# Every fourth expert weight tile split on GpSimd instead of VectorE

## The chip, the cores and the metric

The kernel runs on one core of one Trainium2 chip. The metric is the device time of one execution in microseconds (us); lower is better. A difference of 0.2% (about 4 us) is about what a measurement of this kernel can tell from no change.

Engines, as the profile names them: PE is TensorE (PEld its weight load), DVE is VectorE, ACT is ScalarE, POOL is GpSimd, SP is SyncE, whose queue issues the loads.

## The reference

A decoder trunk of two layers on 256 tokens of width 1024. Each layer has a mixer (a convolution with attention in layer 0, a sparse attention in layer 1) and then a mixer of experts. The experts are where the change lies:

```python
def peer_ffn(h, w_q, sub_keys, u, v):
    ...
        q = (xc @ w_q).reshape(-1, PEER_HEADS, 2, half)
        s = jnp.einsum('thpd,pkd->thpk', q, sub_keys).astype(jnp.float32)
        sv, si = lax.top_k(s, PEER_TOPK)
        ...
        cv, ci = lax.top_k(cand, PEER_TOPK)
        eid = jnp.take_along_axis(cand_id, ci, axis=-1)
        g = jax.nn.softmax(cv, axis=-1)
        ue = u[eid]
        ve = v[eid]
        a = jax.nn.gelu(jnp.einsum('td,thkd->thk', xc, ue)).astype(jnp.float32)
        return jnp.einsum('thk,thkd->td', (g * a).astype(ve.dtype), ve)
```

There are 16,384 experts. For each token eight heads choose 16 of them each.

## The kernel before, in words

The kernel does not gather experts. It multiplies all tokens by all experts, and multiplies the result by a matrix of gates that is zero where an expert was not chosen. So each layer's expert part streams 128 tiles of `peer_u` (first product) and 128 tiles of `peer_v` (second product) through TensorE. One weight tile is 128 x 1024 float32, 512 KB.

Products are made of three TensorE passes, so that they keep nearly float32 precision. `weights` loads a tile into `raw` (5 buffers), then `split` makes two words of it: ACT copies `raw` into `hi` (line 82, rounded to TensorE's format) and DVE writes `lo` = `raw` - `hi` (line 83). `hi` and `lo` have 3 buffers each. The activations have two words too (`h_hi`, `h_lo`), and `over_d` lists, for each of 8 pieces of a tile, the passes hi x h_hi, hi x h_lo and lo x h_hi: 24 matmuls a tile, of which the third is the first that reads `lo`. All of them are recorded at line 100 (`contract`).

The expert part of a layer has these stages, in order of time:

- `score`: the queries and their scores against the keys.
- **Choosing**: `mm1` (first product, tiles 0 to 63, in pairs) runs on TensorE, and meanwhile DVE picks the top 16 of each head (`choose`, lines 740 to 798: searches for maxima and small sums). In layer 0, `ada` (line 149, a product and sum over another streamed tile) runs on DVE too.
- **Gating**: `mm1` for tiles 64 to 127. Between two pairs of tiles `gating` builds the gates of 8 tokens: DVE makes one-hot matrices (`hot`, line 855) and weights them (`w`, line 859), TensorE multiplies them into `pG` (16 matmuls a pair of tiles), and DVE and ACT put them on `S` (lines 838, 869, 871).
- **Second product**: `mm2` for 128 tiles of `peer_v`, which reads `S` through `h_hi` and `h_lo` (lines 885, 886). In layer 0 more of `ada` runs on DVE beside it.

The order of the instructions on each engine is fixed when the program is built: a scheduler runs through the program with its own model of durations and writes for each engine a list, which the engine then follows in that order, waiting where an input isn't ready. So if an instruction moves to another engine, the lists of all engines can change.

GpSimd does next to nothing before the change: a few constants at the start and four fills (lines 529 to 599) ahead of the mixer of layer 1.

Of the kernel before, what the change touches and what calls it, by code (L numbers as in the profile page):

```python
# [7 lines left out]
F32 = mybir.dt.float32  # L8
# [4 lines left out]
ALU = mybir.AluOpType  # L13
# [7 lines left out]
T = 256  # L21
# [23 lines left out]
def terms(a, b):  # L45
    if a.hi is not None and b.hi is not None:
        return [(a.hi, b.hi), (a.hi, b.lo), (a.lo, b.hi)]
    return [(a.raw, b.raw)]
# [3 lines left out]
def trunk(ctx: ExitStack, tc: tile.TileContext, xT, c, ada_w, ada_b, norm_g, even_w, even_wf, even_bf,  # L52
# [3 lines left out]
    V, A, G, PE = nc.vector, nc.scalar, nc.gpsimd, nc.tensor  # L56
# [17 lines left out]
    def load(src):  # L74
        t = st.tile([P, D], F32, tag="raw", bufs=RAW, name="raw")
        nc.sync.dma_start(t, src)
        return t

    def split(raw):
        hi = st.tile([P, D], F32R, tag="hi", bufs=HI, name="hi")  # L80
        lo = st.tile([P, D], F32R, tag="lo", bufs=HI, name="lo")
        A.activation(hi, raw, AF.Copy)  # L82
        V.tensor_tensor(lo, raw, hi.bitcast(F32), op=ALU.subtract)  # L83
        return Op(None, hi, lo)

    meanwhile = [None]

    def weights(src):
        w = split(load(src))
        if meanwhile[0] is not None:  # L90
            meanwhile[0]()
        return w

    def bank(tag, name):
        pool, sizes = ps[0]
        return pool.tile([P, 512], F32, tag=tag, bufs=sizes[tag], name=name)

    def contract(dst, pairs, start=True, stop=True, **kw):
        for n, (a, b) in enumerate(pairs):
            PE.matmul(dst, a, b, start=start and n == 0, stop=stop and n == len(pairs) - 1, **kw)  # L100

    def over_d(w, x, k0=0, k1=KC, order=(0, 1, 2)):

        return [t for k in range(k0, k1)
                for t in map(terms(w.at(lambda a: a[:, k * P:(k + 1) * P]), x.at(lambda a: a[:, k, :])).__getitem__, order)]
# [160 lines left out]
    def project2(src, i, h, name, first=False):  # L266

        p = bank("a", name)
        if first:
            steps(p, [weights(src[i + s]) for s in range(2)], h, range(KC))  # L270
            return p
        for s in range(2):
            contract(p[:, s * T:(s + 1) * T], over_d(weights(src[i + s]), h))
        return p

    def project_t(src, i, h, dst, p=None, qs=range(4)):

        p = p or [bank("y", f"pv{t}") for t in range(2)]
        for q in qs:
            w = weights(src[i + q])  # L280
            for t in range(2):
                for k in range(2):
                    contract(p[t], terms(h.at(lambda a: a[:, 2 * q + k, t * P:(t + 1) * P]),
                                         w.at(lambda a: a[:, k * 512:(k + 1) * 512])),
                             start=(q == 0 and k == 0), stop=(q == 3 and k == 1))
        if 3 in qs:
            for t in range(2):
                A.activation(dst[:, t], p[t], AF.Copy)
        return p
# [399 lines left out]
    def peer(l, early, late, after=None):  # L689
        pp = tc.alloc_tile_pool(name="peer", bufs=1, reuse_waits="tile")  # L690
        hi, lo = (pp.tile([P, KC, T], F32R, name=f"h_{n}") for n in ("hi", "lo"))
        s0 = tc.alloc_tile_pool(name="s0", bufs=1, side="right", reuse_waits="tile")
        S = [s0.tile([P, 64, T], F32, name="S0"), pp.tile([P, 64, T], F32, name="S1")]
        if True:
            h = norm(l, 1, hi, lo, S[0][:, :KC], S[1][:, :KC],
                     [pp.tile([P, T], F32, tag=f"g{n}", bufs=2, name=f"h_t{n}") for n in range(2)], PEER)
# [128 lines left out]
            def mm1(j):  # L825


                p = bank("a", "pmm1")
                for s in range(2):
                    contract(p[:, s * T:(s + 1) * T], over_d(weights(peer_u[l, j + s]), h))  # L830
                p = p.rearrange("p (a t) -> p a t", a=2)
                s = S[j // 64][:, j % 64:j % 64 + 2]
                n = gated[0]
                if n < T:
                    A.activation(s[:, :, n:], p[:, :, n:], AF.Gelu_apprx_tanh)
                if n > 0:
                    A.activation(p[:, :, :n], p[:, :, :n], AF.Gelu_apprx_tanh)
                    V.tensor_tensor(s[:, :, :n], s[:, :, :n], p[:, :, :n], op=ALU.mult)
# [37 lines left out]
            def mm2(j):  # L876
                if j == 0:
                    for n in range(4):
                        yb[n] = bank("y", f"y{n}")
                vx = []  # L880
                for n in range(2):
                    s = S[j // 64][:, j % 64 + n]
                    v = weights(peer_v[l, j + n])
                    x = Op(None, h.hi[:, (j + n) % KC], h.lo[:, (j + n) % KC])
                    A.activation(x.hi, s, AF.Copy)  # L885
                    V.tensor_tensor(x.lo, s, x.hi.bitcast(F32), op=ALU.subtract)  # L886
                    vx.append((v, x))
                order = [(n, k) for n in range(2) for k in range(KC)]
                for n, k in order if j < 126 else sorted(order, key=lambda o: o[1]):
                    v, x = vx[n]  # L890
                    contract(yb[k // 2][:, (k % 2) * T:(k % 2 + 1) * T],
                             terms(v.at(lambda a: a[:, k * P:(k + 1) * P]), x),
                             start=(j + n == 0 and k % 2 == 0), stop=(j + n == 127), skip_group_check=True)
# [22 lines left out]
            for j in range(0, 64, 2):  # L916
                mm1(j)
                for _ in range(2):
                    next(side, None)
                if j >= start:  # L920
                    for f in lots[(j - start) // 2]:
                        f()
            for _ in side:
                pass
            for b in range(32):
                for _ in range(2):
                    gating(64 + 2 * b)
                mm1(64 + 2 * b)
            exps()
            for b, fs in enumerate(spread(early[20:], 32)):  # L930
                mm2(2 * b)
                for f in fs:
                    f()
            s0.release()
            got = None
            for b, fs in enumerate(spread(late, 32)):
                mm2(64 + 2 * b)
                if b == 4:
                    cur[0] = x_tile()
                    nc.sync.dma_start(cur[0], xd)  # L940
                if b == 8 and after is not None:
                    got = after()
                for f in fs:
                    f()
# [130 lines left out]
```

## Time and profile before

| | |
|---|---|
| median of 3 runs | 1990.32 us (1986.63 to 1990.45) |
| the profiled execution, its own time | 1991.12 us |
| its span in the trace | 1989.3 us |
| TensorE busy | 1930.3 us (97%) |
| VectorE busy | 1468.0 us (74%) |
| ScalarE busy | 939.3 us (47%) |
| GpSimd busy | 3.6 us |

Busy is the share of the span in which an engine had an instruction under way. The ends of matmuls are modelled, so the starts of successive matmuls say more of TensorE's pace than its busy share does. [...]

### The profile page before, as it was taken

To read this page: it belongs to the slowest core of one execution; us is meant where nothing else is said; L and a number is where in the kernel's file an instruction comes from. 1 tells how busy PE (TensorE), PEld (TensorE's weight loads), DVE (VectorE), ACT (ScalarE), POOL (GpSimd) and SP (SyncE) were. 2 spreads that over 40 slices of the span, in tenths; PEclk is the share of its full clock that TensorE was granted. 3 is DMA by queue.
4 is the path that set the end of the run, shared out by engine and by line. 5 is a ranking of instruction groups with operands and counts; after the bars stand their busy time and mean duration, and the time that the engine had idled before them with its cause. 6 is when DMAs were issued, how large, how long until landed. Compare 5 with 4: busy or idle time off the path is not lost.

```text
span 1989.3 us, 39878 instructions
## 1 busy us (share of the span) xinstructions
PE 1930.3 (97%) x15994; PEld 1859.0 (93%) x15994; DVE 1468.0 (74%) x3424; ACT 939.3 (47%) x1547; POOL 3.6 (0%) x13
## 2 busy tenths in 40 slices
PE   4899999999999999999999989999999999999999
PEld 3788999999999999999987679999999999999999
DVE  7676999789997666666656859975899975555554
ACT  3445444444444444444456654454444444444443
POOL 0000000000000000000000000000000000000000
PEclk8999999999999999999999999999999999999999
DMA  8866567855455777877743135555554555555554
GB/s 309 262 215 193 177 202 258 273 162 159 150 159 191 233 236 249 294 244 238 228 129 99 41 115 165 177 187 178 159 159 156 154 176 183 181 183 186 183 181 127
DMA packets 105621, 375.44 MB, mean 189 GB/s; under 512 B 12715, under 2 KB 16860, under 8 KB 104540
## 3 DMA queue, kind: packets, MB, share of 16 engines
q1 hardware_dynamic: 104860, 372.38, 58.0%
q8 instruction: 125, 2.05, 0.4%
q10 hardware_dynamic: 576, 0.52, 0.1%
q14 instruction: 60, 0.49, 0.1%
HBM read 369.16 MB, written 6.31 MB: 189 GB/s over the span
## 4 chain that ended last, share of the span: by engine, by line
PE 53%; issue 41%; DMA 3%; DVE 2%; ACT 1%; DVEq 0%; POOL 0%; POOLq 0%; ACTq 0%; SPq 0%
PE pmm L100 19%; PE y L100 19%; PE po L100 2%; DMA raw<-in_ada_w_dram 2%; PE pG L100 1%; PE pq L100 1%; PE pcc L100 1%; PE pwq L100 1%; PE s L638 1%; PE pv L100 1%; DMA S<-in_keys_dram 1%; PE pt L342 1%; PE po_att L653 1%; DMA raw<-in_even_w_dram 1%; PE pb L100 1%
## 5 line engine op out<-in xcount | busy, mean ns | idle before, releaser
L82 ACT ACTIVATE hi<-raw 128x1024 fp32r<-128x1024 f32 x588 | 622.1, 1059 | 899.2 <-PE pmm L100 416.3
L83 DVE TENSOR_TENSOR lo<-raw,hi 128x1024 fp32r<-128x1024 f32 x588 | 717.5, 1221 | 332.2 <-ACT hi L82 331.0
L100 PE MATMUL y<-h_hi,hi 128*128 128x256 f32 x2048 | 579.7, 284 | 6.6 <-ACT h_hi L885 6.6
L100 PE MATMUL pmm<-h_hi,hi 128*128 128x256 f32 x2048 | 584.6, 286 | 0.0
L100 PE MATMUL pmm<-h_hi,lo 128*128 128x256 f32 x2048 | 581.9, 285 | 0.7 <-DVE lo L83 0.7
L100 PE MATMUL pmm<-h_lo,hi 128*128 128x256 f32 x2048 | 582.1, 284 | 0.0
L100 PE MATMUL y<-h_lo,hi 128*128 128x256 f32 x2048 | 580.7, 284 | 0.0
L100 PE MATMUL y<-h_hi,lo 128*128 128x256 f32 x2048 | 578.9, 284 | 0.0
L100 PEld LDWEIGHTS y<-h_hi,hi 128*128 128x128 f32 x2048 | 394.4, 193 | 7.0 <-ACT h_hi L885 7.0
L100 PEld LDWEIGHTS y<-h_lo,hi 128*128 128x128 f32 x2048 | 395.2, 193 | 0.0
L100 PEld LDWEIGHTS y<-h_hi,lo 128*128 128x128 f32 x2048 | 394.0, 193 | 0.0
L100 PEld LDWEIGHTS pmm<-h_hi,lo 128*128 128x128 f32 x2048 | 391.8, 192 | 1.4 <-DVE lo L83 0.9
L100 PEld LDWEIGHTS pmm<-h_lo,hi 128*128 128x128 f32 x2048 | 392.5, 192 | 0.5
L100 PEld LDWEIGHTS pmm<-h_hi,hi 128*128 128x128 f32 x2048 | 392.5, 192 | 0.0
L149 DVE CUSTOM_DVE_ANT_0 raw<-raw,silu 128x1024 f32<-128x1024 f32 x96 | 117.2, 1223 | 93.3 <-DMA raw<-in_ada_w_dram 93.0
L859 DVE TENSOR_TENSOR w<-hot 128x512 f16<-128x512 f16 x256 | 102.8, 418 | 12.4 <-PE pG L100 12.2
L886 DVE TENSOR_TENSOR h_lo<-S,h_hi 128x256 fp32r<-128x256 f32 x256 | 106.0, 418 | 3.2 <-ACT h_hi L885 3.2
L855 DVE TENSOR_TENSOR hot<-hot,lane 128x512 f16<-128x512 f16 x256 | 104.9, 417 | 0.0
L885 ACT ACTIVATE h_hi<-S 128x256 fp32r<-128x256 f32 x256 | 101.6, 402 | 5.5 <-PE y L100 5.5
L100 PE MATMUL pG<-w,hot 128*128 128x128 f16 x1024 | 84.6, 221 | 0.0
L869 DVE TENSOR_TENSOR S<-S,pG 128x256 f32<-128x256 f32 (+5 forms) x252 | 80.1, 347 | 5.0 <-PE pG L100 4.9
L100 PEld LDWEIGHTS <-hot 128*128 128x128 f16 x1024 | 59.2, 98 | 6.8
(269 smaller groups left out, 1845.3 us busy)
## 6 DMA issues: line engine op xcount, KB each, us to landing
raw<-in_peer_u_dram SPq DMA_DIRECT2D x256, 512.0 KB, 3.6
raw<-in_peer_v_dram SPq DMA_DIRECT2D x256, 512.0 KB, 4.2
raw<-in_ada_w_dram SPq DMA_DIRECT2D x96, 512.0 KB, 4.5
raw<-in_even_w_dram SPq DMA_DIRECT2D x24, 512.0 KB, 4.6
raw<-in_odd_w_dram SPq DMA_DIRECT2D x20, 512.0 KB, 4.3
raw<-in_w_q_dram SPq DMA_DIRECT2D x16, 512.0 KB, 4.2
raw<-in_even_wo_dram SPq DMA_DIRECT2D x8, 512.0 KB, 3.5
raw<-in_odd_wo_dram SPq DMA_DIRECT2D x8, 512.0 KB, 3.5
```

The costliest lines, as they stand in the source:

```text
L82: A.activation(hi, raw, AF.Copy)
L83: V.tensor_tensor(lo, raw, hi.bitcast(F32), op=ALU.subtract)
L100: PE.matmul(dst, a, b, start=start and n == 0, stop=stop and n == len(pairs) - 1, **kw)
L149: V.tensor_tensor_reduce(out=w, in0=w, in1=silu, op0=ALU.mult, op1=ALU.add, scale=1.0, scalar=0.0, accum_out=mods[:, l, m:m + 1])
L342: PE.transpose(pt[:, n * P:(n + 1) * P], p[:, n * P:(n + 1) * P], ident)
L638: PE.matmul(s[half][:, x:x + n + pad], qT[r, ch, t * P:(t + 1) * P], k[r, gp, :n + pad], start=True, stop=True)
L653: PE.matmul(po[r, :T], vt[:, 0, cs[half]], pt[half][:, :T], start=(b == 0), stop=False)
L855: V.tensor_tensor(pairs(x), words(v), pairs(lane[:, None].to_broadcast([P, 4, P])), op=ALU.is_equal)
L859: V.tensor_tensor(pairs(x), pairs(o), words(g), op=ALU.mult)
L869: V.tensor_tensor(s[:, :n], s[:, :n], p[:, 64 * f:64 * f + n], op=ALU.mult)
L885: A.activation(x.hi, s, AF.Copy)
L886: V.tensor_tensor(x.lo, s, x.hi.bitcast(F32), op=ALU.subtract)
```

## The change

For the tiles whose number within the layer's `peer_u` or `peer_v` is 3, 7, 11, ..., 127, the subtraction that makes `lo` is issued on GpSimd (`G`) instead of VectorE (`V`). That is 32 tiles of each product in each of two layers, 128 instructions in all. The tiles of the mixers and of the queries stay on VectorE.

```diff
-    def split(raw):
+    def split(raw, pool=False):
         hi = st.tile([P, D], F32R, tag="hi", bufs=HI, name="hi")
         lo = st.tile([P, D], F32R, tag="lo", bufs=HI, name="lo")
         A.activation(hi, raw, AF.Copy)
-        V.tensor_tensor(lo, raw, hi.bitcast(F32), op=ALU.subtract)
+        (G if pool else V).tensor_tensor(lo, raw, hi.bitcast(F32), op=ALU.subtract)
         return Op(None, hi, lo)
...
-    def weights(src):
-        w = split(load(src))
+    def weights(src, pool=False):
+        w = split(load(src), pool)
...
-                    contract(p[:, s * T:(s + 1) * T], over_d(weights(peer_u[l, j + s]), h))
+                    contract(p[:, s * T:(s + 1) * T], over_d(weights(peer_u[l, j + s], (j + s) % 4 == 3), h))
...
-                    v = weights(peer_v[l, j + n])
+                    v = weights(peer_v[l, j + n], (j + n) % 4 == 3)
```

The lists of the engines change in three places that the prediction speaks of. In all the rows below, a number behind a name tells buffers of one name apart.

First, GpSimd's own list, from its last constant of the start (`jp`) on. Before:

```order
L357 IOTA jp_101 128x256
L529 MEMSET ks_11876 128x2x16
L535 MEMSET tcb_11884 128x480
L539 MEMSET gv_11888 128x512
L599 MEMSET pc0_11893 128x128
```

After:

```order
L357 IOTA jp_101 128x256
L83 TENSOR_TENSOR lo_2089<-raw_2086,hi_2088 128x1024
L83 TENSOR_TENSOR lo_2230<-raw_2227,hi_2229 128x1024
L83 TENSOR_TENSOR lo_2370<-raw_2367,hi_2369 128x1024
L83 TENSOR_TENSOR lo_2514<-raw_2511,hi_2513 128x1024
```

Layer 0's 64 subtractions now stand ahead of the fills for layer 1's mixer, and layer 1's 64 behind them; nothing else is on this list.

Second, VectorE's list while layer 0 is choosing, from the subtraction of one tile (`lo_2776`) on; `S1_1602` is the scratch space of the search, `psc0` and `psc1` are banks of scores. Before:

```order
L83 TENSOR_TENSOR lo_2776<-raw_2773,hi_2775 128x1024
L798 TENSOR_TENSOR S1_1602<-S1_1602 128x16x2x2 x2
L741 MATCH_REPLACE S1_1602<-S1_1602,psc1_1863 128x128
L743 MAX_INDEX S1_1602<-S1_1602,psc1_1863 128x8
L742 MAX S1_1602<-S1_1602 128x8
L83 TENSOR_TENSOR lo_2806<-raw_2803,hi_2805 128x1024
L742 MAX S1_1602<-S1_1602 128x8
L149 ISA raw_2911,mods_68<-raw_2911,silu_63 128x1024
L149 ISA mods_68 128x1
L744 MAX_INDEX S1_1602<-S1_1602 128x8
L775 TENSOR_TENSOR S1_1602<-S1_1602 128x128
```

After:

```order
L83 TENSOR_TENSOR lo_2776<-raw_2773,hi_2775 128x1024
L742 MAX S1_1602<-S1_1602 128x8 x2
L744 MAX_INDEX S1_1602<-S1_1602 128x8
L149 ISA raw_2911,mods_68<-raw_2911,silu_63 128x1024
L149 ISA mods_68 128x1
L744 MAX_INDEX S1_1602<-S1_1602 128x8
L741 MATCH_REPLACE S1_1602<-S1_1602,psc0_1949 128x128
L743 MAX_INDEX S1_1602<-S1_1602,psc0_1949 128x8
L740 MAX S1_1602<-psc0_1949 128x8
L783 TENSOR_SCALAR S1_1602<-S1_1602 128x64
L784 TENSOR_SCALAR S1_1602<-S1_1602 128x64
```

The subtraction of `lo_2806` is gone from here, and work of the search that stood later (the scores of `psc0_1949`, of the last two heads) has moved up into its place. The same is so at the other tiles that went to GpSimd.

Third, TensorE's list while layer 0 is gating, at the border of two pairs of tiles; `pG_4935` and `pG_4953` are the two gate products of this border, `pmm1_4965` is the next pair of tiles. Before:

```order
L100 MATMUL pG_4935<-w0_4931,hot_4182 128x128
L100 LDWEIGHTS hot_4182
L100 MATMUL pG_4935<-w1_4933,hot_4182 128x128
L100 MATMUL pmm1_4965<-h_hi_1596,hi_4968 128x256
L100 MATMUL pmm1_4965<-h_lo_1597,hi_4968 128x256
L100 LDWEIGHTS hot_4182
L100 MATMUL pG_4953<-w0_4949,hot_4182 128x128
```

After:

```order
L100 MATMUL pG_4935<-w0_4931,hot_4182 128x128
L100 LDWEIGHTS hot_4182
L100 MATMUL pG_4935<-w1_4933,hot_4182 128x128
L100 LDWEIGHTS hot_4182
L100 MATMUL pG_4953<-w0_4949,hot_4182 128x128
```

The two matmuls of the next pair no longer stand between the two gate products. Over both layers, the 1024 matmuls into `pG` stand in 158 unbroken groups before and in 77 after.

## Rows read from the trace of the kernel before

**Rows 1.** The page, busy time, share of the span and instructions of each engine.

```profile
PE 1930.3 (97%) x15994; PEld 1859.0 (93%) x15994; DVE 1468.0 (74%) x3424; ACT 939.3 (47%) x1547; POOL 3.6 (0%) x13
```

**Rows 2.** Waits of the span: waiter, waited for, us in total, times, longest.

```profile
PE pmm L100 <- DVE lo L83: 0.7, 1, 0.7
...
DVE lo L83 <- ACT hi L82: 331.0, 277, 4.6
```

**Rows 3.** Windows: stretch, length, each engine's busy us (instructions), granted clock, DMA share, GB/s.

```profile
205.00:350.00 145.00, 144.30 (x1192) 143.08 (x1191) 140.09 (x511) 65.43 (x75) 0.00 (x0) 1.00 0.66 211
395.00:620.00 225.00, 225.00 (x2113) 221.59 (x2110) 209.81 (x483) 102.52 (x193) 0.00 (x0) 1.00 0.50 159
625.00:1000.00 375.00, 375.00 (x3118) 373.56 (x3117) 243.60 (x345) 176.49 (x262) 0.00 (x0) 0.99 0.73 242
1200.00:1310.00 110.00, 110.00 (x909) 108.98 (x908) 108.09 (x434) 48.51 (x56) 0.00 (x0) 1.00 0.54 174
1395.00:1615.00 220.00, 216.69 (x2033) 213.12 (x2032) 202.57 (x468) 101.86 (x194) 0.00 (x0) 1.00 0.50 158
1625.00:1985.00 360.00, 360.00 (x3003) 360.00 (x3001) 192.86 (x247) 166.37 (x241) 0.00 (x0) 1.00 0.56 176
```

**Rows 4.** Groups on DVE by form, of the span: busy us, mean ns, idle before.

```profile
L83 DVE TENSOR_TENSOR lo<-raw,hi 128x1024 fp32r<-128x1024 f32 x588 | 717.5, 1221 | 332.2 <-ACT hi L82 331.0
...
L855 DVE TENSOR_TENSOR hot<-hot,lane 128x512 f16<-128x512 f16 x256 | 104.9, 417 | 0.0
```

**Rows 5.** Timeline of ACT, copies into hi: start us, duration us.

```profile
226.23 1.06 ACT L82 ACTIVATE hi<-raw 128x1024 fp32r<-128x1024 f32 x1 [1.82 <-PE pmm L100]
...
229.11 1.06 ACT L82 ACTIVATE hi<-raw 128x1024 fp32r<-128x1024 f32 x1 [1.34 <-PE pmm L100]
...
234.87 1.06 ACT L82 ACTIVATE hi<-raw 128x1024 fp32r<-128x1024 f32 x1 [1.33 <-PE pmm L100]
```

**Rows 6.** Timeline of DVE, the subtractions for the first and last of these.

```profile
228.25 1.20 DVE L83 TENSOR_TENSOR lo<-raw,hi 128x1024 fp32r<-128x1024 f32 x1
...
237.79 1.20 DVE L83 TENSOR_TENSOR lo<-raw,hi 128x1024 fp32r<-128x1024 f32 x1
```

**Rows 7.** Timeline of PE, gating of layer 0, two borders of pairs.

```profile
443.64 0.62 PE L100 MATMUL pG<-w,hot 128*128 128x128 f16 x8
444.06 0.36 PE L100 MATMUL pmm<-h_hi,hi 128*128 128x256 f32 x1
444.27 0.28 PE L100 MATMUL pmm<-h_lo,hi 128*128 128x256 f32 x1
444.39 0.62 PE L100 MATMUL pG<-w,hot 128*128 128x128 f16 x8
444.82 0.36 PE L100 MATMUL pmm<-h_hi,lo 128*128 128x256 f32 x1
445.02 0.28 PE L100 MATMUL pmm<-h_hi,hi 128*128 128x256 f32 x1
...
471.43 1.07 PE L100 MATMUL pG<-w,hot 128*128 128x128 f16 x16
472.31 0.36 PE L100 MATMUL pmm<-h_hi,lo 128*128 128x256 f32 x1
472.51 0.28 PE L100 MATMUL pmm<-h_hi,hi 128*128 128x256 f32 x1
```

**Rows 8.** Groups on POOL by form.

```profile
L138 POOL IOTA lanes<- 128x512 f16 x1 | 1.2, 1197 | 0.0
...
L539 POOL MEMSET gv<- 128x512 f32 x1 | 0.5, 527 | 0.0
```

**Rows 9.** Timelines of POOL and of DVE, start of the program.

```profile
1.02 1.20 POOL L138 IOTA lanes<- 128x512 f16 x1
...
1.49 0.80 DVE L136 TENSOR_SCALAR ident<-ident 128x128 f32<-128x128 f32 x1
...
3.19 0.22 DVE L363 TENSOR_SCALAR cm<-jp 128x128 f32<-128x128 f32 x1
```

## The prediction

> **What bounds the kernel now.** I read the engines' shares first. TensorE is busy for 97% of the span, VectorE for 74%, GpSimd for nothing [rows 1]. The reader is to see that the engine which is relieved is not the one that is full. The list of waits asks the next question: does TensorE ever wait for the subtraction that is moved? In the expert products it does so once, for 0.7 us; the subtraction itself waits 331 us for its input [rows 2]. So taking 128 subtractions off VectorE can give TensorE back about 0.7 us of waiting. The table of stretches shows where VectorE is nevertheless full: 140.1 of 145 us and 108.1 of 110 us while it chooses, 209.8 of 225 us and 202.6 of 220 us while it builds gates, but only 243.6 of 375 us and 192.9 of 360 us beside the second product [rows 3]. In all six stretches TensorE runs at its upper clock and practically without a gap. The stretches that are full on both engines are the ones where this change can do something.
>
> How late may a subtraction be? ScalarE's copies into hi start 2.88 us apart, one a tile, each when TensorE frees a buffer [rows 5]. With three buffers TensorE comes to that tile two tiles later, 5.76 us after the copy's start, and reads lo with its third matmul, 0.24 us more. Of these 6.0 us the copy takes 1.06, so lo must be there 4.9 us after hi. VectorE's subtraction that followed the copy of 226.23 ended at 229.45, 2.8 us ahead of that limit; the one behind the copy of 234.87 ended at 238.99, 1.9 us ahead [rows 5, 6].
>
> **The change, part by part.**
>
> *Relief.* 128 subtractions of 1.22 us, some 156 us, leave VectorE [rows 4]. TensorE's waits for it were 0.7 us, so this alone is worth nothing: I put 0.
>
> *TensorE's list.* In the gating stage the gate products now stand in 77 groups, not 158. The first matmul of a tile behind such a group holds TensorE for 0.20 to 0.21 us (444.06 to 444.27, 444.82 to 445.02, 472.31 to 472.51) where others start 0.12 us apart (444.27 to 444.39). Against that one group of sixteen takes 0.88 us and two of eight 0.42 and 0.43 [rows 7]. So a group less is worth about 0.07 us, and 81 of them 5.7 us: **-5.7 us**. It is a gain only while TensorE doesn't wait there.
>
> *The subtraction on GpSimd.* No row shows it. GpSimd's fill of 512 columns took 0.53 us, its counting pattern of 512 columns 1.20 us [rows 8]; doubled to 1024 columns that is 1.05 to 2.4 us. I take 2.4, because the subtraction also computes each element and has to read two operands first, which the fill doesn't. By itself it is hidden: 2.4 us against 4.9 us leaves 2.5 us, and one VectorE instruction of 1.22 us in its way still leaves 1.3. [...] GpSimd's list holds nothing else that is urgent: the four fills for the mixer of layer 1 come behind layer 0's last subtraction, which is done while the second product still runs.
>
> *VectorE beside a busy GpSimd.* This is the disputed cost. The only row where a VectorE instruction on SBUF data met a long GpSimd instruction is at the start: a 128x128 operation began at 1.49 us, in the middle of GpSimd's pattern (1.02 to 2.22), and lasted 0.80 us, to 2.29; one of the same shape took 0.22 us later, with GpSimd idle [rows 9]. It looks like an instruction that could not proceed until GpSimd had finished. [...]
>
> Choosing: the scheduler has filled the freed slots with later search work, so VectorE's list is as dense between two subtractions as before, with no allowance for a block. I went through the new list from each of the 19 moved tiles that fall in this stage (10 and 9), with the durations of the rows, and took GpSimd's 2.4 us from the end of hi. [...] That gives 0 to 2.2 us, 1.3 in the mean: 25 us. VectorE's idle time in the two stretches takes 4.9 + 1.9 of it, and the lead of 1.9 to 2.8 us can be used up once in each: 25 - 6.8 - 4.7 = **+13 us**, from 0 (GpSimd at 1.05 us, or no block) to 35 (2.4 us each, less the same 11). Behind a late subtraction stand the next tile's subtraction and ada, and with ada the release of raw buffers and so SP's next loads.
>
> Gating: 32 moved subtractions. Nearly everything on VectorE here has two SBUF operands, so the block is about 2 us: 64 us. Against it stand 15.2 + 17.4 us idle, 32 x 1.15 us = 37 us of relief, less the 5.7 us by which TensorE is to become faster: 64 us. That is even, but the 2 us come in one piece, in front of gate products for whose inputs VectorE has about as much in hand (it needs some 3.4 us of the 5.8 us between two groups). I put **+5 us**, 0 to 16 (half a microsecond each).
>
> Second product: 64 moved subtractions, VectorE at 54 to 65%, so a block of 2.4 us in four tiles (11.5 us) fits: 0, while the 4.9 us hold.
>
> Sum: -5.7 + 13 + 5 = +12.3 us. The profiled execution took 1991.1 us (span 1989.3 and 1.8 around it), 0.8 above the median of the runs: 1990.3 + 12.3 = about **2003 us**.
>
> **Rivals.**
>
> *No block* (faster). If the two engines don't hold each other up, the subtraction is hidden in 4.9 us, VectorE has slack everywhere, and only TensorE's shorter list is left: 1990.3 - 5.7 = 1985 us. For it speaks that the one row of a block is another operation; against it that the row ends 0.07 us behind GpSimd's end. It decides from a block of under about 0.4 us in the choosing stage.
>
> *Blocked, but absorbed* (no change). GpSimd at the fill's pace of 1.05 us, or a scheduler's list that happens to put one-operand searches beside GpSimd: then the choosing stage loses some 4 to 8 us and gating nothing, which the 5.7 us pay for: 1989 to 1994 us.
>
> *GpSimd is late itself* (much slower). Were its subtraction, with its own waits for VectorE, longer than 4.9 us, then TensorE would wait at every moved tile, in the second product too: 128 us for each microsecond beyond; at 5.5 us, 77 us: 2068 us. Against it speaks that twice the counting pattern is 2.4 us; for it, that in the gating stage VectorE leaves hardly a gap to GpSimd.
>
> **How the numbers follow.** Forecast 0.58, no block 0.20, absorbed 0.12, GpSimd late 0.10. Differences under 0.2% (4 us) are about what a measurement of this kernel can't tell from no change. The forecast's own range, with the bounds of its terms, is 1995 to 2032. Faster: the no-block case, 0.20. No change: absorbed, 0.12, and the low edge of the forecast, 0.02. Slower: 0.66. The range of 1984 to 2030 holds the no-block case and most of the forecast; outside lie the late GpSimd and the forecast's upper tail.
>
> **What would show it.** Right: VectorE's two-operand instructions that start while GpSimd is busy last longer than their usual 0.42 or 1.22 us and end when it ends; TensorE shows waits for lo while choosing, and waits for w or lo while gating; the second product keeps its pace of 2.88 us a tile; the first matmul behind a gate group still takes 0.20 us, but there are half as many. Wrong: VectorE's durations unchanged (then no block), GpSimd's subtractions over 4.9 us, or waits of TensorE in the second product.

## The result, and the profile after

The changed kernel takes 2015.5 us (median of 4 runs, 2007.88 to 2020.69), the kernel before 1990.38 us beside it (1986.63 to 1992.07). The ratio is 1.0126, 95% interval 1.009 to 1.0162: some 25 us slower. The forecast was 2003; the measured time lies inside the stated range of 1984 to 2030. The profiled execution of the changed kernel is the slowest of the four (2020.69 us, span 2018.9), so what follows from its trace adds up to the 29.6 us between the two spans, not to 25.

The engines' shares and the groups by form, after. They answer to [rows 1] and [rows 4]; two groups that [rows 4] doesn't hold stand first, as they were before.

Before:

```profile
L149 DVE CUSTOM_DVE_ANT_0 raw<-raw,silu 128x1024 f32<-128x1024 f32 x96 | 117.2, 1223 | 93.3 <-DMA raw<-in_ada_w_dram 93.0
L886 DVE TENSOR_TENSOR h_lo<-S,h_hi 128x256 fp32r<-128x256 f32 x256 | 106.0, 418 | 3.2 <-ACT h_hi L885 3.2
```

After:

```profile
PE 1937.3 (96%) x15994; PEld 1865.1 (92%) x15994; DVE 1502.0 (74%) x3296; ACT 945.1 (47%) x1547; POOL 329.9 (16%) x141
...
L83 DVE TENSOR_TENSOR lo<-raw,hi 128x1024 fp32r<-128x1024 f32 x460 | 579.3, 1261 | 230.2 <-ACT hi L82 226.3 <-issue 0.3
...
L83 POOL TENSOR_TENSOR lo<-raw,hi 128x1024 fp32r<-128x1024 f32 x128 | 326.3, 2549 | 1666.4 <-ACT hi L82 1470.6 <-DVE lo L83 54.1 <-DVE S L869 44.0
L886 DVE TENSOR_TENSOR h_lo<-S,h_hi 128x256 fp32r<-128x256 f32 x256 | 190.9, 752 | 51.8 <-ACT h_hi L885 51.7
L149 DVE CUSTOM_DVE_ANT_0 raw<-raw,silu 128x1024 f32<-128x1024 f32 x96 | 136.9, 1429 | 147.6 <-DMA raw<-in_ada_w_dram 105.9 <-issue 41.6
L855 DVE TENSOR_TENSOR hot<-hot,lane 128x512 f16<-128x512 f16 x256 | 133.1, 536 | 0.0
```

The reader is to see that VectorE has 128 instructions fewer and is nevertheless busy 34 us longer. What left it, 128 x 1.22 = 156 us [rows 4], came back as longer durations of other instructions: 190 us in all. `h_lo` went from 418 to 752 ns (85 us over its 256), `hot` from 417 to 536 ns (30 us), the product and sum of ada from 1223 to 1429 ns (20 us), `lo` itself from 1221 to 1261 ns (18 us).

TensorE's waits in the expert products, after, to be held against [rows 2]:

```profile
PE pmm L100 <- DVE lo L83: 22.6, 12, 4.3
...
PE y L100 <- DVE lo L83: 3.6, 6, 0.9
PE pmm L100 <- DVE S L838: 2.8, 2, 1.4
...
PE y L100 <- DVE h_lo L886: 0.8, 1, 0.8
```

All name VectorE; none names GpSimd, whose subtraction takes 2.55 us in the mean. The word that TensorE waits for is one that VectorE still makes.

Where the 29.6 us lie shows when the stages are measured on TensorE's own rows: from the first matmul of tile 0 to that of tile 64 (24 a tile), from there to the first matmul of the second product, and from there to its last. In us, layer 0 / layer 1; the kernels of the experiments stand below in the order in which they are told.

```
                              choosing        gating         second product
before                      191.9 / 190.9   220.2 / 220.2   371.0 / 370.1
after                       212.3 / 202.7   215.7 / 215.8   374.7 / 368.5
e1  choosing only           212.3 / 199.6   220.2 / 220.2   371.4 / 370.0
e2  gating only             190.9 / 190.9   215.7 / 215.8   369.5 / 368.5
e3  second product only     190.9 / 190.9   220.2 / 220.2   372.9 / 370.1
e4  fill                    196.8 / 190.9   214.1 / 214.1   368.7 / 368.5
e5  copy                    196.5 / 191.3   214.1 / 214.0   368.5 / 368.5
e12 two operands, no hi     210.6 / 195.2   214.1 / 214.1   369.5 / 368.5
e10 choosing without ada    199.4 / 199.3   219.7 / 220.2   386.1 / 370.1
e7  grouped, no GpSimd      190.1 / 190.9   218.0 / 217.2   371.1 / 370.1
e8  gating, every second    190.9 / 190.9   218.0 / 218.0   369.8 / 368.5
e11 gating without the last 190.9 / 190.9   214.1 / 214.1   368.5 / 368.5
```

Choosing lost 20.4 and 11.8 us, gating gained 4.5 and 4.4, the second product lost 3.7 and gained 1.6, and what stands ahead of, between and behind the stages of the two layers lost 4.2 together: +32.2 - 8.9 + 2.1 + 4.2 = 29.6.

**A hold-up in the choosing stage.** Rows of the timeline after (start us, duration us), of VectorE and GpSimd, with TensorE's next wait behind them:

```profile
257.09 1.20 DVE L83 TENSOR_TENSOR lo<-raw,hi 128x1024 fp32r<-128x1024 f32 x1
257.31 3.25 POOL L83 TENSOR_TENSOR lo<-raw,hi 128x1024 fp32r<-128x1024 f32 x1 [10.89 <-ACT hi L82]
258.21 0.29 DVE L740 MAX8 S<-psc 128x8 f32<-128x128 f32 x1
258.43 2.31 DVE L787 CAST S<-S 128x128 f16<-128x128 uint32 x1
...
264.80 0.28 PE L100 MATMUL pmm<-h_lo,hi 128*128 128x256 f32 x1
265.63 1.20 DVE L83 TENSOR_TENSOR lo<-raw,hi 128x1024 fp32r<-128x1024 f32 x1
266.89 0.39 PE L100 MATMUL pmm<-h_hi,lo 128*128 128x256 f32 x1 [1.81 <-DVE lo L83]
```

GpSimd's instruction starts in the middle of VectorE's subtraction and takes 3.25 us, 0.85 more than its usual 2.40: here it is GpSimd that was held up, and of its 2.40 us 2.27 lie behind the end of VectorE's subtraction (258.29). Then VectorE's cast, usually 0.30 us, takes 2.31 and ends 0.18 us behind GpSimd (260.74 against 260.56). The search for maxima between them takes its usual 0.29. VectorE is 2 us late from there on, its next subtraction starts at 265.63, and TensorE stands for 1.8 us in front of `lo`.

**The same in the other two stages**, and the rows behind it:

```profile
631.30 2.40 POOL L83 TENSOR_TENSOR lo<-raw,hi 128x1024 fp32r<-128x1024 f32 x1 [10.44 <-ACT hi L82]
631.48 3.30 DVE L83 TENSOR_TENSOR lo<-raw,hi 128x1024 fp32r<-128x1024 f32 x1
634.70 0.64 DVE L838 TENSOR_TENSOR S<-S,pmm 128x480 f32<-128x480 f32 x1
635.40 0.38 PE L100 MATMUL pmm<-h_hi,hi 128*128 128x256 f32 x1 [1.42 <-DVE S L838]
...
1707.44 2.40 POOL L83 TENSOR_TENSOR lo<-raw,hi 128x1024 fp32r<-128x1024 f32 x1 [9.12 <-ACT hi L82]
1707.64 2.48 DVE L886 TENSOR_TENSOR h_lo<-S,h_hi 128x256 fp32r<-128x256 f32 x1 [1.57 <-ACT h_hi L885]
1710.22 1.23 DVE L83 TENSOR_TENSOR lo<-raw,hi 128x1024 fp32r<-128x1024 f32 x1
```

The subtraction that starts in GpSimd's ends at 634.78, 1.08 us behind it: not much less than its own 1.22 us. `h_lo`, 0.42 us by itself, ends 0.28 us behind. So what a hold-up cost here is nearly the rest of GpSimd's instruction: 2.08 us of the 2.22 that were left at 631.48, 2.06 of the 2.20 left at 1707.64.

**The largest stall**, in layer 0 while choosing:

```profile
355.02 5.62 SPq L76 DMA_DIRECT2D raw<-in_peer_u_dram  x2
358.99 0.28 PE L100 MATMUL pmm<-h_lo,hi 128*128 128x256 f32 x1
359.06 1.23 DVE L149 CUSTOM_DVE_ANT_0 raw<-raw,silu 128x1024 f32<-128x1024 f32 x1 [4.06 <-issue]
360.14 2.34 POOL L83 TENSOR_TENSOR lo<-raw,hi 128x1024 fp32r<-128x1024 f32 x1 [9.22 <-ACT hi L82]
360.21 4.49 DVE L83 TENSOR_TENSOR lo<-raw,hi 128x1024 fp32r<-128x1024 f32 x2
363.62 0.58 PE L100 MATMUL pmm<-h_hi,lo 128*128 128x256 f32 x1 [4.35 <-DVE lo L83]
364.00 0.41 PE L100 MATMUL pmm<-h_hi,hi 128*128 128x256 f32 x1
```

VectorE has been idle for 4.06 us in front of an ada product, while SP's queue shows 5.62 us for two loads (what released VectorE the profile doesn't name); then the two subtractions behind it meet GpSimd's and take 4.49 us instead of 2.4. TensorE stands for 4.6 us, and behind the wait its matmuls start 0.21 us apart where they started 0.12 apart. The stretches around it, with the columns of [rows 3], show why:

```profile
359.00:363.60 4.60, 0.27 (x3) 0.07 (x1) 4.54 (x4) 1.01 (x1) 2.34 (x1) 0.78 0.55 184
363.60:366.00 2.40, 2.38 (x11) 2.38 (x12) 1.10 (x1) 0.00 (x0) 0.00 (x0) 0.50 0.56 160
366.00:368.00 2.00, 2.00 (x11) 2.00 (x11) 0.72 (x1) 0.00 (x0) 0.00 (x0) 0.50 0.85 287
368.00:372.00 4.00, 4.00 (x34) 4.00 (x33) 1.86 (x4) 2.14 (x3) 0.00 (x0) 0.95 0.66 199
```

Behind the wait TensorE has a granted clock (the share of its full speed, as the profile gives it) of 0.50 for some 4.4 us, where [rows 3] has 0.99 to 1.00. Over the whole choosing stage of layer 0 TensorE's waits (starts of successive matmuls over 0.3 us apart, each less the usual 0.12) sum to 16.8 us (9 of them), of layer 1 to 8.0 us (4), against 0.9 (1) and none before. Its other starts add 4.7 and 3.9 us to 0.12 us each, against 0.2 and 0.1 before; 6.4 us of that lie in stretches with a granted clock of 0.50. That is 23.9 + 8.3 = 32.2 us, all that the stages lost.

### The profile page after: what moved, and what is told of

Its sections match the earlier page's. It is cut to its first block, busy times and chain, and to the rows that moved or that the text cites. A ratio compares the mean times of both kernels' runs of the same rounds, so it can differ in the third digit from the quotient of the medians.

```text
span 2018.9 us, 40008 instructions
## 1 busy us (share of the span) xinstructions
PE 1937.3 (96%) x15994; PEld 1865.1 (92%) x15994; DVE 1502.0 (74%) x3296; ACT 945.1 (47%) x1547; POOL 329.9 (16%) x141
## 4 chain that ended last, share of the span: by engine, by line
PE 41%; DVE 10%; issue 1%; ACT 0%; DVEq 0%; ACTq 0%
PE y L100 21%; PE pmm L100 10%; DVE lo L83 2%; PE pq L100 1%; PE po L100 1%; PE pG L100 1%; PE s L638 1%; DVE hot L855 1%; PE po_att L653 1%; DVE S L869 1%; DVE w L859 1%; DVE S L744 1%; DVE S L741 1%; PE pt L342 1%; DVE S L743 1%
## 5 line engine op out<-in xcount | busy, mean ns | idle before, releaser
L83 DVE TENSOR_TENSOR lo<-raw,hi 128x1024 fp32r<-128x1024 f32 x460 | 579.3, 1261 | 230.2 <-ACT hi L82 226.3
L83 POOL TENSOR_TENSOR lo<-raw,hi 128x1024 fp32r<-128x1024 f32 x128 | 326.3, 2549 | 1666.4 <-ACT hi L82 1470.6
L100 PE MATMUL y<-h_hi,hi 128*128 128x256 f32 x2048 | 572.8, 283 | 0.0
L149 DVE CUSTOM_DVE_ANT_0 raw<-raw,silu 128x1024 f32<-128x1024 f32 x96 | 136.9, 1429 | 147.6 <-DMA raw<-in_ada_w_dram 105.9
L886 DVE TENSOR_TENSOR h_lo<-S,h_hi 128x256 fp32r<-128x256 f32 x256 | 190.9, 752 | 51.8 <-ACT h_hi L885 51.7
L855 DVE TENSOR_TENSOR hot<-hot,lane 128x512 f16<-128x512 f16 x256 | 133.1, 536 | 0.0
L859 DVE TENSOR_TENSOR w<-hot 128x512 f16<-128x512 f16 x256 | 116.0, 469 | 6.4 <-PE pG L100 6.4
L869 DVE TENSOR_TENSOR S<-S,pG 128x256 f32<-128x256 f32 (+19 forms) x252 | 84.0, 349 | 0.0
L100 PE MATMUL pG<-w,hot 128*128 128x128 f16 x1024 | 70.6, 220 | 0.0
```

Source lines behind the costliest of these rows:

```text
L83: (G if pool else V).tensor_tensor(lo, raw, hi.bitcast(F32), op=ALU.subtract)
L149: V.tensor_tensor_reduce(out=w, in0=w, in1=silu, op0=ALU.mult, op1=ALU.add, scale=1.0, scalar=0.0, accum_out=mods[:, l, m:m + 1])
L855: V.tensor_tensor(pairs(x), words(v), pairs(lane[:, None].to_broadcast([P, 4, P])), op=ALU.is_equal)
L859: V.tensor_tensor(pairs(x), pairs(o), words(g), op=ALU.mult)
L869: V.tensor_tensor(s[:, :n], s[:, :n], p[:, 64 * f:64 * f + n], op=ALU.mult)
```

## The experiments

Theory 1: GpSimd's subtraction and VectorE's instructions hold each other up, as in the rows above (the cast 2.31 us for 0.30, GpSimd's subtraction 3.25 for 2.40); it is GpSimd's reading that does it, and the time that VectorE is held up comes out where VectorE has no slack, that is while choosing. Rivals: the second word is late because GpSimd starts it late or is slow; or not GpSimd's work but the other order of the instructions, which the scheduler writes when a subtraction moves, makes and loses the time. All ratios are to the kernel before, run beside.

**One stage at a time.** Three kernels move the subtractions of one stage alone: e1 the tiles below 64 of the first product, e2 those from 64 on, e3 the second product.

```diff
-  over_d(weights(peer_u[l, j + s]), h)
+  over_d(weights(peer_u[l, j + s], (j + s) % 4 == 3 and j < 64), h)    # e1
+  over_d(weights(peer_u[l, j + s], (j + s) % 4 == 3 and j >= 64), h)   # e2
...
+  v = weights(peer_v[l, j + n], (j + n) % 4 == 3)                      # e3
```

> Only the 32 moved tiles of the choosing stages (tiles 3 to 63 of the first product, both layers) stay on GpSimd. Theory 1 (the cost arises in the choosing stages, where VectorE's list has no slack for being held up): about the whole loss of the change is here, before plus 25 to 33 us, 2015 to 2023 us; the choosing stages take some 20 and 12 us longer and the others are as before. Rival (each moved tile costs alike, wherever it is): a quarter of the loss, plus 6 to 8 us, 1997 us.

> Only the 32 moved tiles of the gating stages (tiles 67 to 127 of the first product) stay on GpSimd; TensorE's list then has 74 unbroken groups of gate matmuls against 158. Theory 1: a gain here, minus 9 us as the two gating stages of the changed kernel show, about 1982 us, though VectorE is held up in them just as often. Rival (each moved tile costs alike): plus 6 to 8 us, 1997 us. Rival (no gain from groups, gating unchanged): 1990 us.

> Only the 64 moved tiles of the second product stay on GpSimd. Theory 1: VectorE has room, so nearly nothing: plus 0 to 4 us, 1990 to 1994 us. Rival (each moved tile costs alike): half of the loss, plus 12 to 15 us, 2004 us.

Measured: e1 2016.85 us (1.0118, 1.01 to 1.0137), e2 1980.11 us (0.9943, 0.9927 to 0.996), e3 1995.08 us (1.0025, 1.0015 to 1.0035). Against the 1990.66 us beside them: +26.2, -10.5, +4.4. So the loss is made in the choosing stage, with 32 of the 128 moved subtractions; in the gating stage, where the forecast's terms left a gain of 0.7 us, the change gains ten; the second product, which I had put at nothing, costs a little, just over the 0 to 4 us that I had expected of e3. In e3 1.9 us of it lie in the second product of layer 0 and 2.6 in the mixer of layer 1. That mixer holds none of the moved subtractions, and in every other version too it is longer than in the kernel before, by 0.7 to 3.0 us (e7, without GpSimd, 0.8); so its length can't be put down to the moved subtractions, and its cause is open.

**What GpSimd must do to hold VectorE up.** Two kernels move the same 128 tiles as the change, but GpSimd writes something else into `lo`: in e4 zeros, which read nothing, in e5 a copy of `raw`, which reads one operand. In e4 the second word of these tiles is left out of the products; in e5 `raw` itself stands in its place.

```diff
-  V.tensor_tensor(lo, raw, hi.bitcast(F32), op=ALU.subtract)
+  if pool:
+      G.memset(lo.bitcast(F32), 0.0)     # e4
+      G.tensor_copy(lo, raw)             # e5 instead
+  else:
+      V.tensor_tensor(lo, raw, hi.bitcast(F32), op=ALU.subtract)
```

> As the changed kernel, but for its 128 tiles GpSimd fills lo with zeros instead of subtracting (the low word of these weights is left out of the products). GpSimd writes as much and reads nothing, and takes about 1.05 us instead of 2.4. Theory 1 (VectorE is held up by GpSimd's reading): VectorE's instructions keep their durations beside it, no waits for lo while choosing, and the shorter list of gate groups (74) is left: 1983 to 1987 us. Rival 2 (the scheduler's rearranged lists by themselves cost the time, with no holding up): a loss of the same kind remains, 2005 to 2020 us. Rival 3 (GpSimd holds VectorE up whatever it does): shorter blocks, plus 0 to 10 us, 1990 to 2000 us, with VectorE's instructions lengthened by up to 1.05 us.

> As the changed kernel, but for its 128 tiles GpSimd copies raw into lo instead of subtracting (one operand read instead of two; lo of these tiles then holds raw itself). Theory 1 (GpSimd's reading holds VectorE up for as long as GpSimd's instruction lasts): VectorE's instructions with two SBUF operands stretch here too, by at most this copy's length; if the copy takes 1 to 1.3 us, the choosing stages lose 5 to 12 us together, against 32 before, and with the gain in the gating stages the total is 1984 to 1996 us. Rival (only an operation with two operands holds VectorE up): no stretched instructions, as with the fill, 1982 us. Rival (one operand is as slow as two): 2.4 us and 2010 to 2020 us.

Measured: e4 1981.83 us (0.9957, 0.994 to 0.9974), e5 1981.26 us (0.9939, 0.9923 to 0.9956). Rows of the timeline of e4 (VectorE's subtraction stands at line 86 there, GpSimd's fill at 84):

```profile
228.45 1.23 DVE L86 TENSOR_TENSOR lo<-raw,hi 128x1024 fp32r<-128x1024 f32 x1
228.46 0.96 POOL L84 MEMSET lo<- 128x1024 f32 x1 [10.55 <-PE pmm L103]
...
265.10 1.22 DVE L86 TENSOR_TENSOR lo<-raw,hi 128x1024 fp32r<-128x1024 f32 x1
265.61 0.95 POOL L84 MEMSET lo<- 128x1024 f32 x1 [10.38 <-PE pmm L103]
```

Fills (0.95 to 0.96 us) and subtractions (1.22 to 1.23) lie beside each other and both keep their time. A cast with one operand that began 0.33 us before a fill's end did not; it took 0.51 us for its usual 0.30.

```profile
1290.34 0.95 POOL L84 MEMSET lo<- 128x1024 f32 x1 [10.56 <-PE pmm L103]
1290.96 0.51 DVE L791 CAST S<-S 128x128 f16<-128x128 uint32 x1
```

In e5, with the copy:

```profile
314.29 1.87 POOL L84 CAST lo<-raw 128x1024 fp32r<-128x1024 f32 x1 [10.45 <-PE pmm L103]
315.60 1.63 DVE L86 TENSOR_TENSOR lo<-raw,hi 128x1024 fp32r<-128x1024 f32 x1
```

Here the subtraction ends 1.07 us behind GpSimd's copy: it was held up, as in the changed kernel (1.63 us for 1.22). But the copy takes 1.24 us in the mean, and it needs no `hi`, so it starts as soon as TensorE frees the buffer. It meets VectorE's two-operand work seldom and briefly: `hot` takes 441 ns in the mean, not 536, and the choosing stages lose 4.6 and 0.3 us. So in these rows GpSimd's reading of one operand was enough to hold up a VectorE instruction with two (1.63 us), and its writing alone was not (1.22 to 1.23). The totals don't tell the two theories apart: e4 came out 1 us under the range that I had given it, e5 under that of Theory 1 (1984 to 1996) and at the rival's 1982; the durations decide. In layer 0 e4 loses 4.9 us of choosing with 0.1 us of hold-ups: there VectorE waits 38.7 us for ada's loads between 205 and 430 us, against 9.8 in the kernel before. That part may come of the changed order or of when the buffers come free; no run separates these.

**Length, or the late start?** e5 is both shorter and earlier than the subtraction. In e12 GpSimd subtracts `raw` from itself: two operands, and still no `hi`.

```diff
-      G.tensor_copy(lo, raw)
+      G.tensor_tensor(lo, raw, raw, op=ALU.subtract)
```

> All 128 tiles of the change go to GpSimd again, but there it subtracts raw from itself: lo is filled with zeros, so the second word of these tiles is left out. It reads two operands for the whole length of the instruction, as the change does, and needn't wait for hi, so it starts earlier, like the copy that read one operand (1.24 us, the choosing stages 4.6 and 0.4 us longer than before). Theory 1 (what costs is how long VectorE is held up): the instruction takes 2.4 us, and the choosing stages lengthen by 8 to 20 us each where the copy cost 4.6 and 0.4; the time is 1995 to 2015. Rival (what costs is that the subtraction starts behind hi, in the middle of VectorE's work for the next tile, and lo is late on either engine): with the early start the choosing stages stay within 5 us of the copy's, and the time is 1980 to 1987.

Measured: 2000.98 us (1.0056, 1.0038 to 1.0074). GpSimd's instruction took 2.07 us in the mean, not 2.4. The choosing stages lost 18.7 and 4.3 us, 14.1 and 4.0 more than with the copy. TensorE's waits for the subtraction of VectorE are back:

```profile
PE pmm L103 <- DVE lo L86: 14.8, 11, 4.1
```

So with the same early start the longer instruction brings most of layer 0's loss back, and Theory 1 carries it. The closer comparison is with e4, because there the order can't be the cause: VectorE's 3296 instructions stand in the same order in e4 and e12 but for some 20, and in layer 1's choosing stage TensorE's 1615 matmuls do so without exception. With the fill these stages took 196.8 and 190.9 us, with the subtraction 210.6 and 195.2. In layer 1 the increase is under the 8 us that I had given as its lower end, and 7.5 us less than in the changed kernel: there the start behind `hi`, or the last half microsecond of length, does the rest. These two aren't told apart. In the gating stages no stall is left (214.1).

**Choosing without ada.** The choosing stage of layer 0 lost 8.6 us more than that of layer 1, and its largest stall stood behind an ada product. e10 is e1 with the ada products of that stage moved into the second product.

```diff
-                if j >= start:
-                    for f in lots[(j - start) // 2]:
-                        f()
...
-            for b, fs in enumerate(spread(early[20:], 32)):
+            for b, fs in enumerate(spread(early, 32)):
```

> Moved tiles in the choosing stages only, as in the first experiment, and layer 0's ada tiles are taken out of its choosing stage (they run beside its second product instead). Layer 0 lost 20 us there and layer 1, which has no ada, 12 us or less. If the difference comes from ada (an operand-pair instruction more, and loads that come late behind held-up buffers): layer 0's choosing stage loses about what layer 1's does, 8 to 12 us, and the whole is 2004 to 2012 us. If the loss has nothing to do with ada: 2013 to 2020 us as before.

Measured: 2021.01 us (1.0142, 1.0122 to 1.0162). Both choosing stages now take the same, 199.4 and 199.3 us: the 12.9 us that e1 loses more in layer 0 go with ada. Not all of them need a hold-up, as e4's 4.9 us in this stage show, and the kernel before with ada moved out was not run. The total isn't lower, because the second product of layer 0, with all of ada in it, takes 386.1 us, 14.8 more than in e1; my expectation of the total missed that.

Side by side, the hold-ups and what they cost. For the first column, each VectorE instruction that overlaps one of GpSimd's counts with its duration less the median of its form in the kernel before, if that is over 0.06 us. In us, the choosing stages, layer 0 / layer 1:

```
          hold-ups on VectorE    stage longer than before
e4        0.1 /  0.3              4.9 /  0.0
e5        6.8 /  2.6              4.6 /  0.3
e12      14.8 / 10.7             18.7 /  4.3
e10      12.5 / 13.6              7.5 /  8.4
e1       22.1 / 13.6             20.4 /  8.7
after    23.1 / 14.6             20.4 / 11.8
```

In the second product of the changed kernel the hold-ups are larger, 46.5 and 59.8 us, and that stage lost 3.7 us and gained 1.6: VectorE had the time there (54 to 65% busy before [rows 3]).

**Where the gating stage's gain comes from.** e7 has no subtraction on GpSimd at all; it writes the gating stage so that the two groups of gate products between two pairs of tiles come in one piece, as the changed kernel's list has them: 90 groups, where before has 158 and the change 77.

```diff
-            def gating(j):
+            def gating(j, b):
...
-                b = gated[0] // 4
...
+                yield
...
-                    contract(p[:, t], [(a[:, t], x[:, t]) for x in w])
+                    contract(p[:, t], [(a[:, t], x[:, t]) for x in w[::-1]])
...
-                for _ in range(2):
-                    gating(64 + 2 * b)
+                gs = [gating(64 + 2 * b, 2 * b + n) for n in range(2)]
+                for g in gs + gs[::-1]:
+                    next(g, None)
```

> The kernel before, with every subtraction on VectorE; only the gating code is written in another order, so that the gate matmuls stand in 90 unbroken groups instead of 158. If the gain in the gating stages comes from the order of TensorE's list alone: 0.06 us for each of 68 groups is 4 us, and if the wait of 3.3 us at the start of each second product goes with it another 6.6: 1980 to 1987 us. If the gain needs VectorE relieved by GpSimd: no change or slower, 1989 to 1996 us, with waits of TensorE for the gates' inputs.

Measured: 1985.65 us (0.997, 0.9955 to 0.9984), so 6.6 us faster with the order alone. What the gating stage of the kernel before also has is one wait at its end, ahead of the second product. Its rows, and the stretches around it:

```profile
622.38 1.28 ACT L110 ACT_TABLE_LOAD   x1
624.21 0.58 PE L100 MATMUL y<-h_hi,hi 128*128 128x256 f32 x1 [3.31 <-ACT h_hi L885]
```

```profile
620.60:624.20 3.60, 0.29 (x3) 0.09 (x1) 1.96 (x5) 3.36 (x6) 0.00 (x0) 0.81 0.81 292
624.20:627.00 2.80, 2.79 (x13) 2.80 (x14) 2.80 (x8) 2.16 (x8) 0.00 (x0) 0.50 1.00 404
```

ScalarE is behind with the last copies, TensorE stands, and goes on at a granted clock of 0.50: 3.6 us in the gating stage of each layer and 2.5 and 1.6 us of slower starts in the second product. In the changed kernel ScalarE starts the first `h_hi` at 639.42, TensorE comes to it at 641.25, and this wait is gone. In e7 it is still there, with 2.4 us; less the 2.6 us that it costs there, e7's gating stages take 215.4 and 214.5 us, against 216.6 in the kernel before less its 3.6: 1.2 and 2.1 us for 34 groups fewer a layer, 0.05 us each.

**More of it in the gating stage.** e8 moves every second tile there, 64 instead of 32, and nothing elsewhere (`s == 1 and j >= 64`).

> Only in the gating stages, but every second tile on GpSimd (64 moved subtractions instead of 32). Theory 1: VectorE is held up 2 to 2.4 us per moved tile and relieved of 1.15, so twice the tiles cost it some 64 x 1 us more against 32 us idle time left in the two stages; no further gain, and from 1980 us a loss of 0 to 15 us: 1980 to 1995 us. Rival (relief of VectorE is what helped): a further gain of 5 us or more, 1975 us.

Measured: 1985.02 us (0.9968, 0.9954 to 0.9982), 218.0 us a gating stage where e2 takes 215.8. `hot` takes 736 ns in the mean, GpSimd's subtraction 2.84 us, and there are two stalls of 1.3 to 1.4 us a layer instead of one. So here more relief of VectorE is a loss.

**The one stall of the gating stage.** In the changed kernel and in e2 a gating stage takes 215.7 to 215.8 us, 1.6 to 1.7 more than in e4, where nothing is held up in this stage. The rows above show one place for it: TensorE's wait of 1.42 us at 635.40, behind the moved subtraction of tile 127. e11 is e2 without that one.

```diff
-  over_d(weights(peer_u[l, j + s], (j + s) % 4 == 3 and j >= 64), h)
+  over_d(weights(peer_u[l, j + s], (j + s) % 4 == 3 and 64 <= j < 126), h)
```

> Only the gating stage's moved subtractions remain, as in the run with gating alone, but the last one of each layer (tile 127) goes back to VectorE. Account A (the hold-ups in the gating stage cost time in one place only, the stall of 1.42 us in front of the last two tiles, behind that subtraction): the stall is gone in both layers, a gating stage takes 214.1 us instead of 215.6, and the time is some 3 us below 1980.1, about 1977. Account B (the stall belongs to the end of the stage, where the last gate groups and the last copies crowd, whoever subtracts): it stays, 215.6 us and 1980, or it is larger, since VectorE has 1.22 us more there.

Measured: 1974.07 us (0.9921, 0.9908 to 0.9935), beside 1988.53 us for the kernel before. Both gating stages take 214.1 us, and TensorE shows no gap there, at a granted clock of 1.00:

```profile
395.00:600.00 205.00, 205.00 (x1951) 203.50 (x1950) 194.14 (x437) 97.81 (x179) 40.68 (x15) 1.00 0.51 160
600.00:620.00 20.00, 20.00 (x185) 19.91 (x185) 18.29 (x38) 12.86 (x27) 0.00 (x0) 1.00 0.63 211
```

The 30 subtractions that are left on GpSimd cost the gating stages nothing; the 2 at tile 127 cost them 3.4 us. Another 1.0 us went in the second product of layer 0, where e2 has one wait of 0.70 us for `h_lo` at the start; that makes the time lower than the 1977 us of Account A. This is the fastest version of the study, 14.5 us faster than the kernel before.

## Why the prediction was right, and where its sizes were off

*What bounds it, and the relief.* Right. TensorE waited for `lo` for 0.7 us before, and there was no wait for `lo` to be removed. The granted clock was 0.99 to 1.00 in all six stretches, the upper clock of the prediction. But TensorE was not without a gap in all of them: in the fifth it was busy for 216.69 of 220 us [rows 3], and the missing 3.3 us are the wait ahead of the second product, which the prediction read past.

*The subtraction on GpSimd.* Right in size (2.40 us undisturbed, as taken) and in its being hidden: no wait of TensorE names GpSimd, so the rival of the late GpSimd is out.

*VectorE beside a busy GpSimd.* That VectorE is held up was right, with some luck: it was read off one row of 0.80 us [rows 9] that shows another pair. There VectorE's operation has one operand and GpSimd's counting pattern reads nothing, so the row doesn't agree in kind with two operands beside a reading GpSimd; in e4, where GpSimd only writes too, two-operand subtractions keep their time (1.22 to 1.23 us) and a cast doesn't (0.51 for 0.30). The no-block rival is out: the instructions did last longer (`h_lo` 752 ns for 418), and e4, with next to no hold-ups, is some 34 us faster than the change; the absorbed case is out with the measured +25. Which of VectorE's instructions go on beside GpSimd no row of the kernel before shows; in the forecast it was my estimate. In the changed kernel 45 searches (`MAX8`, `FIND_INDEX8`, `MATCH_REPLACE8`) began in a subtraction of GpSimd over 0.15 us before its end and took 0.27 to 0.30 us, as before. Of those that began so, the 16 ada products took 2.71 us in the median for 1.23 and the 12 subtractions into `lo` 3.30 for 1.22; but 18 of 44 `hot` and `w` took their usual 0.42 to 0.43, and there GpSimd's subtraction took 3.2 to 3.7 us. And the instructions don't end when GpSimd ends, as the prediction said, but up to 1.08 us later (`lo` 1.08, `h_lo` 0.28). The cast of 258.43, with one operand, was held up for 2 us, and casts of that line take 802 ns in the mean, against 300 before; casts and one operation with a scalar make 6.2 of the 37.7 us of hold-ups in the choosing stages. The row on which I rested had shown it, for the operation of 1.49 us is one with one operand.

*Choosing, +13.* This is the step that was mis-sized: the stages lost 32.2 us in the profiled execution. The working counted blocks at 19 of the 32 moved tiles, up to tile 43 in layer 0 and tile 35 in layer 1, because VectorE had been full up to there. Over this part the stages lost 10.0 and 11.8 us, 21.8 where 13 was forecast, with 29.3 us of hold-ups where the working had 25: the price of a block was near. No run shows the 1.3 us at each of the 19 tiles from which those 25 come; the measured 29.3 are 1.5 each. Behind them layer 1 lost nothing, but layer 0, where ada still ran, another 10.4 us, nearly all at tile 45 (6.7, the largest stall) and tile 58 (3.8). The runs split it in another way. Without ada in the way the two stages lose 7.5 and 8.4 us (e10), 15.9 together, not far from 13. What the working lacked is the queue behind a late VectorE, which the prediction named ("and with ada the release of raw buffers and so SP's next loads") and gave no price: e1 loses 12.9 us more than e10 in layer 0. The remaining 3 us in layer 1 (202.7 against 199.6 in e1) don't come of the order, which is the same on VectorE and TensorE in that stage of both; they weren't followed. TensorE's slower starts, 8.3 us in all and 6.4 of them at a granted clock of 0.50, are inside these numbers and were in none of mine.

*TensorE's list, -5.7.* Right: without its wait the gating stage before took 216.6 us, in e11 214.1, with 42 groups fewer a layer: 0.06 us a group, 5.0 us for both layers. The rows of the prediction give 0.06 too, not 0.07 (two groups of eight with their slow first matmuls against one of sixteen with its own). What I hadn't seen is the wait at the start of the second product, which is gone after the change: 7.2 us in the gating stages and up to 4.0 behind them. With the grouping alone it stays at 2.4 us (e7); whether VectorE's relief or the order of the last instructions removes it wasn't told apart.

*Gating blocks, +5.* Right in size: 1.6 and 1.7 us, 3.4 in all, but in a single place in each layer, as e11 shows, not spread over 32. The price given to each block, about 2 us of VectorE, holds at 631.48 (3.30 us for 1.22), but no run shows the 64 us of blocks in the two stages: counted as in the table above, the changed kernel has 22.2 us of hold-ups in each, 44.4 in all.

*Second product, 0.* Too low: the term is hidden by the gain behind the removed wait. Against e4 the second product of layer 0 is 5.9 us longer, with six short waits for `lo` beside ada and one for `h_lo`; that of layer 1, without ada, is not. Waits of TensorE in this stage were among the prediction's own signs of being wrong; they came, 4.4 us of them, all in layer 0, and they name VectorE's words, not GpSimd's.

So the sum of the terms that I had, -5.7 + 13 + 5, is short by layer 0's choosing beside ada and the slower starts on one side and long by the removed wait on the other. The direction hung on the choosing term being larger than the two gains, which it was. That the time fell inside 1984 to 2030 says little, for the no-block and the absorbed rival lie in that range too (and the forecast's own range, 1995 to 2032, isn't what its bounds add up to, 1985 to 2036). What decides for the mechanism is the durations of VectorE's instructions.

## What to carry to other kernels

Relieving a busy engine is worth no more than the waits for it, 0.7 us here, and if the helper holds it up, as GpSimd did VectorE here, it can take more than it gives: 156 us of relief for 190 us of longer instructions. Price a hold-up at what remains of the helper's instruction (2.08 of 2.22 us at 631.48), and place the helped instructions only where the held engine has slack; one badly placed in 16 can be the whole cost of a stage. When an edit moves instructions, read the new order on every engine, for gains and losses that have nothing to do with what the edit is for: here 6.6 us came with the order alone.

## What the runs showed of the hardware that I had not expected

- A one-operand cast on VectorE was held up for the whole rest of GpSimd's subtraction (2.31 us for 0.30), while a search for maxima beside it kept its time (MAX8 at 258.21, 0.29); and GpSimd is held up by VectorE as well (3.25 us for 2.40).
- GpSimd's fill, which only writes, held up a one-operand cast (0.51 us for 0.30, e4) and not the two-operand subtractions (1.22 to 1.23 us beside a fill).
- A VectorE instruction that was held up wasn't ready when GpSimd ended: `lo` (1024 columns, 1.22 us by itself) ended 1.08 us later, `h_lo` (256 columns, 0.42 us) 0.28 us.
- GpSimd's copy of one 128x1024 operand took 1.04 us undisturbed (e5), its fill 0.95 (e4), its subtraction of `raw` from itself 1.90 (e12), of `hi` from `raw` 2.40 (the changed kernel).
- Behind a wait of 4.6 us TensorE's granted clock was 0.50 for some 4.4 us (363.60 to 368.00); behind one of 2.1 us (264.80 to 266.89) it was 1.00 in the stretch that followed (266.89 to 271.00).
